# Three more pairs of f tiles begun in the norm of the first feed-forward, their sums kept in DRAM

## The chip, the cores and the metric

The kernel runs on one core of a Trainium2 chip. The metric is the device time of one execution in microseconds (us). The engines are named as in the profile: PE is TensorE, PEld its weight load, DVE is VectorE, ACT is ScalarE, POOL is GpSimd, and SP issues nearly all DMAs; SPq is its queue.

## The reference

The block computes, in float32 for one sequence of 1024 positions with a model width of 1024:

```python
x = x + 0.5 * swiglu(rms_norm(x, ffn1_norm), ffn1_w_gate, ffn1_w_up, ffn1_w_down)
h = rms_norm(x, mix_norm)
x = x + concat(rwkv7_mix(h @ w_in), pool_mix(h @ w_in)) @ w_out
x = x + 0.5 * swiglu(rms_norm(x, ffn2_norm), ffn2_w_gate, ffn2_w_up, ffn2_w_down)
out = rms_norm(x, final_norm)
# swiglu(h, g, u, d) = (silu(h @ g) * (h @ u)) @ d, inner width 2816
```

The change touches the first line only: the norm in front of the first feed-forward and its two products with the gate and the up weights.

## The kernel before

**Tiling.** The inner width of 2816 is cut into 22 f tiles of 128, taken as 11 pairs. For a pair, gate and up are each a product of a 2 x 2 block matrix of weights with a 2 x 2 block matrix of the normed input. It is done with seven block products in place of eight, named P1 to P7. The right sides of the seven are forms of the normed input: `b11` and `b21` (two of its blocks), `b22`, and the sums and differences `t1` to `t4`. Every product is float32 out of two halves: `split` writes a high part with an ACT copy and a low part with a DVE subtraction, and `mm3` (lines 252 to 254) then issues three matmuls for each of four blocks of 128 rows. A product is thus 12 matmuls of 128x512, and a pair takes 14 products.

**Order of a pair.** In `gate_up` the first two products (`first`) need only `b11` and `b21`: P1 is copied out of PSUM by ACT as `c1`, and P2 is added to it by DVE as `c11`. The other five (`rest`) need the other forms and add on to `c1`. `store` then multiplies gate with up on POOL and puts seven tiles of the pair into the DRAM tensor `ascr`, for the down product.

**The norm.** `start` makes the forms of the input, in an order that a planner (`Plan`) writes out for all engines: each operation gets a priority from the length of the chain behind it and from a table `LEAD`, which adds a number for each part of the work. The input `x` is loaded as eight tiles of 512 KB, squared and summed (ACT), transposed (PE, line 845), written back transposed to `xtd`, scaled (line 852, which reads `bc`, the row scales spread over the partitions by PE at line 835), and split. The first 512 positions give `b11` and `b21`, the second 512 give the other forms. In between `start` makes P1 and P2 of the first three pairs (`NPRE`): a weight tile `raw` of 512 KB is loaded by two DMAs (line 728), split into two `wf` tiles (lines 705 and 672), and used by two products on `pp_` accumulators, which take turns in a ring of two PSUM banks; line 735 is the ACT copy and line 737 the DVE add. There are three `raw` buffers, eight `wf` and ten `c`.

**The other norm.** In front of the second feed-forward `start` makes P1 and P2 of six pairs. It keeps the sums of the last three as `c1` and `c11` in the DRAM tensor `c1d` (line 741), and `gate_up` reads them back with `kept` (line 447). Sums of five more pairs were put there earlier, so `gate_up` of the second feed-forward computes five products instead of seven for all of its 11 pairs. The first feed-forward has the argument `a_left` false and does all seven for its last eight pairs.

Of the kernel before, what the change touches and what calls it, by code (L numbers as in the profile page):

```python
# [8 lines left out]
F32 = mybir.dt.float32  # L9
# [7 lines left out]
P = 128  # L17
# [3 lines left out]
NF = DFF // P  # L21
KD = D // P
HT = 512
# [12 lines left out]
class Plan:  # L36
# [148 lines left out]
    def lag(self, i, u):  # L185
# [4 lines left out]

LEAD = {"": 48.5, "1e00": 696.8, "1e01": 905.5, "1e10": -2683.6, "1e11": 2081.2, "1e20": -2679.1, "1e21": -2658.5,
# [15 lines left out]

MANUAL = {mybir.EngineType.PE, mybir.EngineType.DVE, mybir.EngineType.Activation, mybir.EngineType.Pool,  # L210
          mybir.EngineType.SP}
# [3 lines left out]
def block_kernel(ctx, tc, x, ffn1_norm, ffn1_w_gate, ffn1_w_up, ffn1_w_down, mix_norm, w_in,  # L215
# [6 lines left out]
    dram = ctx.enter_context(tc.tile_pool(name="dram", bufs=1, space=DRAM))  # L222
# [100 lines left out]
    NPRE = 3  # L323

    NEARLY = 5
    PROD = ("P1", "P2", "P4", "P6", "P7", "P5", "P3")
    PROD2 = ("P1", "P2", "P3", "P6", "P7", "P5", "P4")

# [2 lines left out]

    def gate_up(fp, rf, begun, wg, wu, ascr, a_left, ahead):

# [115 lines left out]
        for i in range(NF // 2):  # L451
            ahead(i)
            qs = []
            for n, src in enumerate((wg, wu)):
                a = loads(src, i) if i + n else blocks
                if (i, n) in early:
                    c1, q = early[i, n], []
                elif a_left:
                    c1, q = kept(0, i, n), [kept(1, i, n)]
                else:  # L460
                    c1, c11 = first(a)
                    q = [c11]
                q += rest(a, c1, None if i + n else made)
                if n == 0:
                    for c in q:
                        silu(c)
                qs.append(q)
            if i == NF // 2 - 1:
                ahead(i + 1)
            store(i, *qs)  # L470

    TAIL = 3
    NPR = NF // 2
# [167 lines left out]
            split(hi[:, k, :], lo[:, k, :], hf, lo_eng="pool" if k % 2 else "dve")  # L641


    def start(fp, rf, wg, wu, ascr, inputs, pre, through, aside=()):

# [5 lines left out]
        PE, DVE, ACT, POOL, SP = "PE", "DVE", "ACT", "POOL", "SP"  # L651
# [130 lines left out]
    x_v = x[0].rearrange("(i p) d -> p i d", p=P)  # L782
    xtd = dram.tile([NH, P, KD, HT], F32, name="xtd")
    x1d = dram.tile([NH, P, KD, HT], F32, name="x1d")
    ascr = dram.tile([7, NF // 2, P, HT], F32, name="ascr")

    DSC = 4 * (16 * L + 16)
# [12 lines left out]
    with tc.tile_pool(name="f12", bufs=2, side="right", reuse_waits="tile") as fp:  # L800
# [4 lines left out]
        rf = {nm: form(nm) for nm in ("b11", "b21", "b22", "t2", "t3", "t4")}  # L805
# [57 lines left out]
                    else:  # L863
                        rest_ops(k, a, b, "xn0" if k == 0 else "")

        begun = start(fp, right, ffn1_w_gate[0], ffn1_w_up[0], ascr, inputs1, "1", {"PE": 4.4, "ACT": 5.8})

        wb = w_blocks(lambda n: xb.tile([P, 8 * HT], F32, tag="x", name="wx") if n == 0 else xtile("wx", [P, 8 * HT]),
                      ffn1_w_down[0], False)
# [8 lines left out]
                for q in range(3):  # L878
                    load_a(fp, 0, q, PROD)

        gate_up(fp, rf, begun, ffn1_w_gate[0], ffn1_w_up[0], ascr, False, ahead1)

        vec_columns([name for name, _, _ in vecs if name != "g1"])
        omu = const.tile([P, 14], F32, name="omu")
# [32 lines left out]
    xbs.close()  # L917

    x2d = dram.tile([P, KD, HT], F32, name="x2d")
    c1d = dram.tile([2, NF // 2, 2, P, HT], F32, name="c1d")  # L920
    x2n = dram.tile([NH, P, 4, D], F32, name="x2n")
    with tc.tile_pool(name="mix", bufs=1, side="right", reuse_waits="tile") as mp_:

# [882 lines left out]
    with tc.tile_pool(name="f34", bufs=2, side="right", reuse_waits="tile") as fp:  # L1806
        def to_natural(i):

            for q in range(2):
                pt = bank("ptn")  # L1810
                for k in range(4):
                    nc.tensor.transpose(pt[:, k * P:(k + 1) * P], x2[:, q * 4 + k, i * P:(i + 1) * P], ident)
                xs = const.tile([P, HT], F32, tag="sq", name="xs", bufs=3)
                nc.scalar.copy(xs, pt)
                nc.scalar.dma_start(x2n[1, :, i, q * HT:(q + 1) * HT], xs)

        rf3.update({nm: form(nm) for nm in ("b22", "t2", "t3", "t4")})
        rf3["t1"] = xb.tile([P, 2, KH, HT], F32R, tag="x", name="t1")


        fp.tile([P, HT], F32, tag="c", name="c", bufs=10)
        def inputs2(plan, E, alloc, ct, st, sq, sub, split_op, rest_ops):
            op = plan.op
            for k in range(KH):
                plan.part = f"2f{k}"
                hs = []
                for m in (k, k + KH):
                    hf = f"hf{m}"
                    op("DVE", 0.66, lambda m=m, hf=hf: nc.vector.scalar_tensor_tensor(
                        ct(hf), x2[:, m, :], col("g3", m), x2rb, op0=ALU.mult, op1=ALU.mult), "", f"{hf} H", [(hf, "c")])  # L1830
                    hs.append(hf)
                rest_ops(k, *hs, "")

        begun = start(fp, rf3.get, ffn2_w_gate[0], ffn2_w_up[0], ascr, inputs2, "2",
                      {"PE": 8.0, "DVE": 8.0, "ACT": 4.0, "POOL": 4.0}, range(NPRE + NEARLY, NPR))

        wb = w_blocks(lambda n: xtile("wx", [P, 8 * HT]),
                      ffn2_w_down[0], True)

        def ahead2(i):  # L1840
            if 1 <= i <= 4:
                to_natural(i - 1)
            if i >= NPR - 2:
                for _ in range(8 if i == NPR - 2 else 4 if i == NPR else 0):
                    wb[1](*wb[2].pop(0))
            if i == NPR:
                for q in range(3):
                    load_a(fp, 0, q, PROD2)

        gate_up(fp, rf3, begun, ffn2_w_gate[0], ffn2_w_up[0], ascr, True, ahead2)  # L1850

        fg = fp.tile([P, D], F32, tag="raw", name="fg", bufs=3)
        xo = []

        def out2(r, c, m):
            if not xo:
                xo.extend([xtile("xo0", [P, 4, D]), xb.tile([P, 4, D], F32, tag="x", name="xo1")])
                nc.scalar.dma_start(fg, final_norm.rearrange("(a d) -> a d", a=1).broadcast_to([P, D]))
            cs = slice(c * HT, (c + 1) * HT)
            return xo[r][:, m, cs], x2n[r, :, m, cs]  # L1860

        def finish(r, t):
            xs = xo[r][:, t, :]
            s = const.tile([P, 2], F32, tag="s", name="s", bufs=3)
            for q in range(2):
                qs = slice(q * HT, (q + 1) * HT)
                junk = const.tile([P, HT], F32, tag="sq", name="junk", bufs=3)
                nc.scalar.activation(junk, xs[:, qs], AF.Square, accum_out=s[:, q:q + 1])
            nc.vector.tensor_scalar(s[:, 0:1], s[:, 0:1], s[:, 1:2], 1.0 / D, ALU.add, ALU.mult)
            nc.vector.tensor_scalar(s[:, 0:1], s[:, 0:1], RMS_EPS, None, ALU.add)  # L1870
            nc.gpsimd.tensor_tensor(s[:, 0:1], s[:, 0:1], mhalf[:, 0:1], op=ALU.pow)
            nc.vector.scalar_tensor_tensor(xs, xs, s[:, 0:1], fg, op0=ALU.mult, op1=ALU.mult)  # L1872
            r0 = (r * 4 + t) * P
            nc.sync.dma_start(out[0, r0:r0 + P, :], xs)

        def after2(n, m):
            if n == "P5":
                finish(0, m)
            if n == "P4":
                finish(1, m)  # L1880

        down(fp, wb, True, out2, after2)
# [25 lines left out]
```

## Time and profile before

| | |
|---|---|
| median of three runs | 1982.69 us (1980.05 to 1983.21) |
| profiled execution | 1979.47 us, of which the span from first to last instruction is 1977.7 us |
| PE busy in the span | 1860.0 us (94%) |
| DVE, ACT, POOL busy | 1356.7, 814.9, 677.5 us |
| mean granted clock of PE | 0.974 of full speed |

Matmuls are pipelined, so a PE that is busy all the time is shown as busy for the whole of a stretch, and the distance between the starts of two matmuls is what one costs. The busy share is a mean over stages: what is looked for is the stretches where PE is not busy, and there what it waits for. In the stretches the columns are the bounds and length of the stretch, then busy time of PE, PEld, DVE, ACT and POOL with the number of instructions, the granted clock, the mean busy share of the 16 DMA engines, and GB/s. In a timeline a bracket gives the idle time ahead of an instruction and what ended it.

### The profile page before, as it was taken

How to read it: one execution, taken by the hardware profiler on the slowest of the kernel's cores; microseconds unless marked ns; L12 is line 12 of the kernel's file. 1: busy time of each engine (PE TensorE's matmuls, PEld its weight loads, DVE VectorE, ACT ScalarE, POOL GpSimd, SP SyncE). 2: the span in 40 equal slices, each digit the busy share in tenths (PEclk: the TensorE clock that was granted, in tenths of full speed). 3: DMA queues.
4: the chain of work that ended last, by engine and by line, in shares of the span. 5: the costliest groups of instructions: out<-in, count | busy, mean ns of one | idle time of the engine just before them, and what ended most of it. 6: DMA issues, size and time to landing. Idle time of an engine off the chain costs nothing.

```text
span 1977.7 us, 28018 instructions
## 1 busy us (share of the span) xinstructions
PE 1860.0 (94%) x10042; PEld 1478.5 (75%) x10042; DVE 1356.7 (69%) x2299; ACT 814.9 (41%) x1410; POOL 677.5 (34%) x589
## 2 busy tenths in 40 slices
PE   6799999999899998988899998898999999998997
PEld 5588888888678776666677776777788888886886
DVE  7965555556888857677787577456855455589876
ACT  7423333323344455455553445244433222243444
POOL 0375665561631112001310010100266777825300
PEclk9899999999899998989999999999999999998999
DMA  9334333236632342232233437335555655484233
GB/s 286 103 125 131 105 109 102 87 111 230 212 106 93 121 116 61 53 69 59 43 72 94 125 82 207 100 97 177 165 196 174 205 171 180 169 277 132 95 101 128
DMA packets 271532, 260.50 MB, mean 132 GB/s; under 512 B 68318, under 2 KB 197666, under 8 KB 271138
## 3 DMA queue, kind: packets, MB, share of 16 engines
q1 hardware_dynamic: 269952, 256.06, 41.8%
q10 hardware_dynamic: 1442, 2.66, 0.4%
q8 instruction: 80, 1.31, 0.3%
q14 instruction: 58, 0.48, 0.1%
HBM read 186.55 MB, written 71.84 MB: 131 GB/s over the span
## 4 chain that ended last, share of the span: by engine, by line
PE 42%; DVE 6%; ACT 2%; issue 1%; DMA 1%; POOL 0%; SPq 0%; POOLq 0%; DVEq 0%; ACTq 0%
PE pw L252 3%; PE pw L253 3%; PE pw L254 3%; PE pst L1434 1%; DVE da L249 1%; DVE xo L1872 1%; DVE xo L561 0%; PE pz L1409 0%; DVE dw L249 0%; DMA tscr<-ti 0%; PE py L1416 0%; PE sc L1258 0%; PE ptt L1366 0%; DVE xo L601 0%; DVE u L1274 0%
## 5 line engine op out<-in xcount | busy, mean ns | idle before, releaser
L245 ACT ACTIVATE wf<-s 128x512 fp32r<-128x512 f32 x172 | 107.6, 631 | 289.3 <-POOL s L386 87.5
L249 DVE TENSOR_TENSOR wf<-s,wf 128x512 fp32r<-128x512 f32 x172 | 155.8, 906 | 61.7 <-ACT wf L245 59.8
L249 DVE TENSOR_TENSOR dw<-wx,dw 128x512 fp32r<-128x512 f32 x132 | 109.0, 826 | 57.5 <-ACT dw L245 57.4
L245 ACT ACTIVATE dw<-wx 128x512 fp32r<-128x512 f32 x132 | 83.1, 630 | 157.6 <-PE pd__4772 L254 16.9
L249 DVE TENSOR_TENSOR wf<-raw,wf 128x512 fp32r<-128x512 f32 x76 | 78.1, 1028 | 70.7 <-ACT wf L245 69.8
L245 ACT ACTIVATE da<-ar 128x512 fp32r<-128x512 f32 x154 | 95.5, 620 | 43.3 <-DMA ar<-ascr 23.7
L529 POOL TENSOR_TENSOR wx<-wx 128x512 f32<-128x512 f32 x44 | 78.4, 1799 | 100.6 <-DMA wx<-in_ffn_w_down_dram 59.8
L249 DVE TENSOR_TENSOR da<-ar,da 128x512 fp32r<-128x512 f32 x132 | 106.1, 804 | 6.3 <-ACT da L245 6.3
L425 POOL TENSOR_TENSOR c<-c,c 128x512 f32<-128x512 f32 x60 | 98.8, 1647 | 33.4 <-DVE c L353 32.5
L392 POOL TENSOR_TENSOR s<-raw 128x512 f32<-128x512 f32 x44 | 57.2, 1300 | 144.5 <-DMA raw<-in_ffn_w_gate_dram 80.6
L984 DVE TENSOR_TENSOR w<-w 128x512 fp32r<-128x512 f32 (+2 forms) x108 | 70.4, 659 | 18.3 <-ACT w L979 9.8
L979 ACT ACTIVATE w<-w 128x512 fp32r<-128x512 f32 (+2 forms) x108 | 62.6, 595 | 48.0 <-DVE w L984 30.8
L245 ACT ACTIVATE wf<-raw 128x512 fp32r<-128x512 f32 x76 | 47.8, 629 | 78.8 <-DMA vrow<-in_mix_norm_dram 6.3
L386 POOL TENSOR_TENSOR s<-s,raw 128x512 f32<-128x512 f32 x42 | 57.4, 1366 | 34.4 <-DVE wf L249 33.7
L403 POOL TENSOR_TENSOR s<-raw,s 128x512 f32<-128x512 f32 x42 | 54.3, 1292 | 40.6 <-DVE wf L249 35.8
L252 PE MATMUL pw<-h2hi,w 128*128 128x512 f32 (+1 forms) x144 | 62.1, 431 | 2.8 <-ACT w L979 2.8
L252 PE MATMUL pw<-h,w 128*128 128x512 f32 (+1 forms) x144 | 63.3, 439 | 0.0
L254 PE MATMUL pw<-h2hi,w 128*128 128x512 f32 (+1 forms) x144 | 59.1, 411 | 2.1 <-DVE w L984 2.0
L1404 ACT ACTIVATE spt<-sv,ep 128x128 f32<-128x128 f32 x60 | 24.1, 401 | 89.1 <-DVE sv L1441 80.0
L409 ACT ACTIVATE c<-c 128x512 f32<-128x512 f32 x74 | 46.7, 631 | 32.4 <-DVE c L353 27.7
L249 POOL TENSOR_TENSOR da<-ar,da 128x512 fp32r<-128x512 f32 x22 | 32.1, 1461 | 79.7 <-ACT da L245 79.7
L384 POOL TENSOR_TENSOR s<-raw 128x512 f32<-128x512 f32 x42 | 56.5, 1345 | 7.5 <-DMA raw<-in_ffn_w_up_dram 2.0
(3084 smaller groups left out, 5935.7 us busy)
## 6 DMA issues: line engine op xcount, KB each, us to landing
ar<-ascr SPq DMA_DIRECT2D x70, 512.0 KB
ascr<-c SPq DMA_DIRECT2D x132, 256.0 KB
raw<-in_ffn_w_gate_dram SPq DMA_DIRECT2D x44, 512.0 KB
wx<-in_ffn_w_down_dram SPq DMA_DIRECT2D x88, 256.0 KB
raw<-in_ffn_w_up_dram SPq DMA_DIRECT2D x44, 512.0 KB
w<-in_w_in_dram SPq DMA_DIRECT2D x64, 256.0 KB
ck<-c1d SPq DMA_DIRECT2D x32, 256.0 KB
w<-in_w_out_dram SPq DMA_DIRECT2D x26, 256.0 KB
```

The source lines that it names most:

```text
L245: nc.scalar.activation(hi, src, AF.Copy)
L249: eng.tensor_tensor(lo, src, hi.bitcast(F32), op=ALU.subtract)
L252: nc.tensor.matmul(acc, lhsT=lhi, rhs=rhi, start=first, stop=False)
L253: nc.tensor.matmul(acc, lhsT=lhi, rhs=rlo, start=False, stop=False)
L254: nc.tensor.matmul(acc, lhsT=llo, rhs=rhi, start=False, stop=last)
L384: nc.gpsimd.tensor_tensor(s1, a21, a22, op=ALU.add)
L386: nc.gpsimd.tensor_tensor(s2, s1, a11, op=ALU.subtract)
L392: nc.gpsimd.tensor_tensor(s3, a11, a21, op=ALU.subtract)
L425: eng.tensor_tensor(u[j], u[j], g[j], op=ALU.mult)
L529: eng.tensor_tensor(out, a, b, op=op)
L979: nc.scalar.activation(part(t, q, kn), by32(raw), AF.Copy)
L984: nc.vector.tensor_tensor(part(E[f"l{w}"], q, kn), by32(raw), part(E[f"h{w}"], q, kn).bitcast(F32), op=ALU.subtract)
```

## The change

P1 and P2 of the pairs 3, 4 and 5 (`NASIDE` = 3) of the first feed-forward are made by `start` as well. Their sums go to a new DRAM tensor `c0d` of the shape of `c1d`, and `gate_up` reads them back with `kept` for these three pairs; the pairs 6 to 10 still do seven products there. The table `LEAD` has new numbers for the parts of the first norm (the names that begin with 1), so the order of all engines is new up to the pair 6; behind it the order on each engine is that of before, but for line numbers and buffer numbers. The instructions of PE, DVE, ACT and POOL are as many as before. SP issues 36 DMAs more, of 256 KB each: 12 loads of weights (the columns of P1 and P2 of the six weight tiles, which `gate_up` loads whole again later), 12 stores to `c0d` and 12 loads from it.

```diff
-LEAD = {"": 48.5, "1e00": 696.8, "1e01": 905.5, "1e10": -2683.6, "1e11": 2081.2, "1e20": -2679.1, "1e21": -2658.5,
+LEAD = {"": 48.5, "1e00": 1988.1, "1e01": 2891.4, "1e11": -36.8, "1e20": -64.8, "1e21": -450.3, "1e30": 1.9,
...
+    NASIDE = 3
...
-    def gate_up(fp, rf, begun, wg, wu, ascr, a_left, ahead):
+    def gate_up(fp, rf, begun, wg, wu, ascr, a_left, ahead, aside, c1d):
...
-                elif a_left:
+                elif i in aside:
                     c1, q = kept(0, i, n), [kept(1, i, n)]
                 else:
                     c1, c11 = first(a)
...
-    def start(fp, rf, wg, wu, ascr, inputs, pre, through, aside=()):
+    def start(fp, rf, wg, wu, ascr, inputs, pre, through, aside, c1d):
...
+    c0d = dram.tile([2, NF // 2, 2, P, HT], F32, name="c0d")
...
-        begun = start(fp, right, ffn1_w_gate[0], ffn1_w_up[0], ascr, inputs1, "1", {"PE": 4.4, "ACT": 5.8})
+        begun = start(fp, right, ffn1_w_gate[0], ffn1_w_up[0], ascr, inputs1, "1", {"PE": 4.4, "ACT": 5.8},
+                      range(NPRE, NPRE + NASIDE), c0d)
...
-        gate_up(fp, rf, begun, ffn1_w_gate[0], ffn1_w_up[0], ascr, False, ahead1)
+        gate_up(fp, rf, begun, ffn1_w_gate[0], ffn1_w_up[0], ascr, False, ahead1, range(NPRE, NPRE + NASIDE), c0d)
```

**First place: SP at the start of the program.** The first loads stand there; `raw` is a weight tile, `xn` the input. Before:

```order
L728 DMA raw<-in_ffn_w_up_dram 128x4x128 x2
L817 DMA xn_106<-in_x_dram 128x1024 x4
L728 DMA raw<-in_ffn_w_up_dram 128x4x128 x2
L728 DMA raw<-in_ffn_w_gate_dram 128x4x128 x2
L817 DMA xn_107<-in_x_dram 128x1024 x2
```

In the change:

```order
L824 DMA xn_108<-in_x_dram 128x1024 x4
L732 DMA raw<-in_ffn_w_up_dram 128x4x128 x2
L824 DMA xn_109<-in_x_dram 128x1024 x3
L858 DMA xtd<-sq 128x512 x3
L824 DMA xn_109<-in_x_dram 128x1024
```

The first four tiles of the input now stand ahead of the first weights, and the loads of two further weight tiles behind the second half of the input.

**Second place: DVE where it comes to the second half of the input.** `bc_313` and `bc_465` are the row scales of that half, `sq` is a transposed tile, `wf` is a weight split, and L737 (now L741) adds a product `pp`. Before:

```order
L672 TENSOR_TENSOR b21_111<-st_309,b21_111 128x512
L672 TENSOR_TENSOR wf_298<-raw_243,wf_298 128x512
L852 SCALAR_TENSOR_TENSOR c_354<-sq_339,vt_86,bc_313 128x512
L672 TENSOR_TENSOR wf_307<-raw_243,wf_307 128x512
L672 TENSOR_TENSOR st_365<-c_354,st_333 128x512
L672 TENSOR_TENSOR wf_350<-raw_254,wf_350 128x512
```

In the change:

```order
L676 TENSOR_TENSOR c_373<-c_373,c_403 128x512
L676 TENSOR_TENSOR wf_417<-raw_365,wf_417 128x512
L676 TENSOR_TENSOR wf_431<-raw_381,wf_431 128x512
L676 TENSOR_TENSOR wf_451<-raw_400,wf_451 128x512
L741 TENSOR_TENSOR c_428<-pp__423,c_428 128x512
L859 SCALAR_TENSOR_TENSOR c_479<-sq_339,vt_86,bc_465 128x512
L676 TENSOR_TENSOR wf_472<-raw_381,wf_472 128x512
L676 TENSOR_TENSOR st_490<-c_479,st_394 128x512
```

The first operation on the second half stood behind the splits of seven `wf` tiles; now 14 such splits and the adds of three products stand ahead of it. On PE the matmuls that make `bc_465` stand behind seven whole products in the change, and the first of them that reads `bc_465` here comes next on DVE.

**Third place: DVE at the end of the norm.** `t2`, `t3` and `t4` are forms, `wf_623` and `wf_875` the weight of the first product of the five that need them; the next rows (L249, now L250) belong to `gate_up`. Before:

```order
L672 TENSOR_TENSOR t2_113<-c_588,t2_113 128x512
L672 TENSOR_TENSOR wf_430<-raw_304,wf_430 128x512
L672 TENSOR_TENSOR t4_115<-st_593,t4_115 128x512
L737 TENSOR_TENSOR c_608<-pp__562,c_559 128x512
L672 TENSOR_TENSOR st_610<-raw_370,raw_408 128x512
L672 TENSOR_TENSOR st_617<-st_610,raw_370 128x512
L672 TENSOR_TENSOR c_535<-c_535,c_608 128x512
L672 TENSOR_TENSOR wf_623<-st_617,wf_623 128x512
L249 TENSOR_TENSOR wf_673<-s3_671,wf_673 128x512
```

In the change:

```order
L676 TENSOR_TENSOR st_684<-st_684,c_718 128x512
L676 TENSOR_TENSOR wf_775<-raw_724,wf_775 128x512
L676 TENSOR_TENSOR t4_117<-st_684,t4_117 128x512
L676 TENSOR_TENSOR st_849<-b21_113 128x512
L676 TENSOR_TENSOR st_849<-st_849,c_749 128x512
L741 TENSOR_TENSOR c_859<-pp__835,c_840 128x512
L676 TENSOR_TENSOR t4_117<-st_849,t4_117 128x512
L676 TENSOR_TENSOR st_870<-st_802,raw_492 128x512
L676 TENSOR_TENSOR wf_875<-st_870,wf_875 128x512
L250 TENSOR_TENSOR wf_915<-s3_913,wf_915 128x512
L250 TENSOR_TENSOR wf_933<-raw_553,wf_933 128x512
L741 TENSOR_TENSOR c_893<-pp__877,c_881 128x512
```

Before, a `wf` of an early product, the last, was split between the last forms, and the adds of two early P2 stood behind the rows shown. In the change the last early weight (from `raw_724`) is split ahead of the last `t4`, and of the adds of the 12 early P2 only the last, of `pp__877`, stands behind `wf_875`.

## Rows read from the trace of the kernel before

**Rows 1.** Page, part 1: busy us (share of the span) xinstructions.

```profile
PE 1860.0 (94%) x10042; PEld 1478.5 (75%) x10042; DVE 1356.7 (69%) x2299; ACT 814.9 (41%) x1410; POOL 677.5 (34%) x589
```

**Rows 2.** Stretches of 10 us of the first feed-forward's norm. Columns: TensorE to GpSimd, clock, DMA.

```profile
0.00:10.00 10.00, 1.19 (x3) 0.54 (x3) 3.36 (x44) 4.40 (x6) 0.83 (x7) 1.00 0.78 244
10.00:20.00 10.00, 6.97 (x34) 6.44 (x34) 4.57 (x8) 9.02 (x18) 1.03 (x1) 1.00 1.06 326
20.00:30.00 10.00, 8.90 (x48) 6.53 (x49) 10.00 (x18) 9.06 (x18) 1.02 (x1) 1.00 1.04 329
...
50.00:60.00 10.00, 8.43 (x34) 5.90 (x33) 10.00 (x18) 4.36 (x8) 0.00 (x0) 1.00 0.15 53
60.00:70.00 10.00, 1.93 (x9) 1.22 (x7) 10.00 (x17) 3.60 (x6) 0.00 (x0) 0.76 0.14 52
70.00:80.00 10.00, 8.43 (x26) 6.43 (x27) 9.06 (x11) 4.01 (x8) 5.98 (x5) 0.72 0.62 186
80.00:90.00 10.00, 10.00 (x45) 8.02 (x44) 9.27 (x11) 4.43 (x8) 5.96 (x5) 1.00 0.47 131
```

**Rows 3.** Stretches of the two gate and up stages, same columns.

```profile
100.00:500.00 400.00, 400.00 (x1712) 322.02 (x1712) 229.53 (x304) 125.06 (x204) 219.35 (x156) 1.00 0.39 128
1510.00:1734.00 224.00, 224.00 (x966) 180.33 (x965) 124.77 (x168) 64.70 (x111) 173.73 (x120) 1.00 0.55 183
```

**Rows 4.** Timeline of TensorE, norm of the first feed-forward. Columns: start us, us, engine line op.

```profile
35.42 1.04 PE L845 MATMUL pt<-ident,xn 128*128 128x128 f32 x8
...
61.54 0.40 PE L254 MATMUL pp__562<-b,wf 128*128 128x512 f32 x1
70.81 0.79 PE L252 MATMUL pp__613<-b,wf 128*128 128x512 f32 x1 [8.87 <-DVE c L737]
...
76.53 0.40 PE L252 MATMUL pp__676<-t,wf 128*128 128x512 f32 x1
77.70 0.50 PE L252 MATMUL pp__635<-b,wf 128*128 128x512 f32 x1 [0.77 <-ACT c L735]
...
80.61 0.40 PE L252 MATMUL pp__656<-t,wf 128*128 128x512 f32 x1
...
85.30 0.39 PE L252 MATMUL pp__694<-t,wf 128*128 128x512 f32 x1
...
88.11 0.40 PE L252 MATMUL pp__712<-t,wf 128*128 128x512 f32 x1
```

**Rows 5.** Timeline of VectorE, the same norm.

```profile
17.58 1.41 DVE L852 SCALAR_TENSOR_TENSOR st<-sq,vt,bc 128x512 f32<-128x512 f32 x2 [1.25 <-PE bc L835]
...
25.75 0.68 DVE L672 TENSOR_TENSOR b<-st,b 128x512 fp32r<-128x512 f32 x1
...
30.15 0.68 DVE L672 TENSOR_TENSOR b<-st,b 128x512 fp32r<-128x512 f32 x1
...
33.54 0.68 DVE L672 TENSOR_TENSOR st<-c,st 128x512 f32<-128x512 f32 x1
...
70.07 0.68 DVE L737 TENSOR_TENSOR c<-pp__562,c 128x512 f32<-128x512 f32 x1
...
73.47 0.69 DVE L672 TENSOR_TENSOR wf<-st,wf 128x512 fp32r<-128x512 f32 x1
```

**Rows 6.** Timeline of all engines, the first loads.

```profile
0.81 1.00 SPq L728 DMA_DIRECT2D raw<-in_ffn_w_up_dram  x2
...
3.82 0.63 ACT L705 ACTIVATE wf<-raw 128x512 fp32r<-128x512 f32 x1 [0.69 <-DMA raw<-in_ffn_w_up_dram]
...
11.93 1.06 ACT L822 ACTIVATE t<-xn 128x1024 fp32r<-128x1024 f32 x1 [0.20 <-DMA xn<-in_x_dram]
```

**Rows 7.** Timeline of TensorE, norm of the second feed-forward.

```profile
1357.52 0.80 PE L252 MATMUL pp__12004<-b,wf 128*128 128x512 f32 x1 [5.03 <-ACT wf L705]
...
1425.96 0.50 PE L252 MATMUL pp__12549<-b,wf 128*128 128x512 f32 x1 [1.12 <-DVE c L737]
...
1428.87 0.40 PE L252 MATMUL pp__12568<-t,wf 128*128 128x512 f32 x1
```

More of the change, by code (lines that the diff above doesn't have):

```diff
@@ L784, in block_kernel @@
     x1d = dram.tile([NH, P, KD, HT], F32, name="x1d")
+    c0d = dram.tile([2, NF // 2, 2, P, HT], F32, name="c0d")
+    c1d = dram.tile([2, NF // 2, 2, P, HT], F32, name="c1d")
     ascr = dram.tile([7, NF // 2, P, HT], F32, name="ascr")
@@ L919, in block_kernel @@
     x2d = dram.tile([P, KD, HT], F32, name="x2d")
-    c1d = dram.tile([2, NF // 2, 2, P, HT], F32, name="c1d")
     x2n = dram.tile([NH, P, 4, D], F32, name="x2n")
@@ L1834, in block_kernel @@
         begun = start(fp, rf3.get, ffn2_w_gate[0], ffn2_w_up[0], ascr, inputs2, "2",
-                      {"PE": 8.0, "DVE": 8.0, "ACT": 4.0, "POOL": 4.0}, range(NPRE + NEARLY, NPR))
+                      {"PE": 8.0, "DVE": 8.0, "ACT": 4.0, "POOL": 4.0}, range(NPRE + NEARLY, NPR), c1d)
         wb = w_blocks(lambda n: xtile("wx", [P, 8 * HT]),
@@ L1848, in ahead2 @@
                     load_a(fp, 0, q, PROD2)
-        gate_up(fp, rf3, begun, ffn2_w_gate[0], ffn2_w_up[0], ascr, True, ahead2)
+        gate_up(fp, rf3, begun, ffn2_w_gate[0], ffn2_w_up[0], ascr, True, ahead2, range(NPRE, NPR), c1d)
         fg = fp.tile([P, D], F32, tag="raw", name="fg", bufs=3)
```

31 rows, old and new, of the table LEAD are left out of this document.

## The prediction

> **What bounds the kernel now.** I read the page's first part, then stretches, then the timelines of PE and DVE where a stretch has a hole. PE is busy 1860.0 us of the span [rows 1]; what can be gained is in the rest and in slow clock. In the gate and up stage of the first feed-forward PE is busy 400.00 of 400.00 us [rows 3]: there each product that is taken out shortens the program by what a product costs. That is 2.81 us, from the start of `pp__694` at 85.30 to that of `pp__712` at 88.11 [rows 4]; 12 matmuls at 400 us for 1712 [rows 3] are 2.804; I reckon with 2.805. In the norm ahead of it the picture is the other way round. From 50 to 80 us DVE is busy 29.06 of 30 us, PE 18.79 [rows 2]; PE waits 8.87 us for a DVE add ahead of `pp__613`, and the granted clock is 0.76 and 0.72 in the two stretches around that hole [rows 2, 4], with matmuls of 0.79 us where others take 0.40 [rows 4].
>
> I measure the norm by what PE has lost by its end: the time less 2.805 us for each product done. At 80.61 us, when `pp__656`, the first product whole on a new form, starts and PE has no more holes [rows 2 to 4], 12 early products and 4 of the 12 matmuls of `pp__676` (the last of them at 76.53 [rows 4]) are done: 80.61 - 12.33 x 2.805 = **46.0 us lost**.
>
> **What the change does.** Nothing is removed in sum. 12 products (12 x 2.805 = 33.7 us of PE) move from a stage that PE bounds into one where it waits. With them go 12 high and 12 low weight halves, 6 ACT copies and 6 DVE adds, from a stage where DVE is busy 229.53 of 400 us [rows 3] into one that DVE bounds. In the norm DVE issues a row each 0.619 us (59 rows of its order from 33.54 to 70.07 [rows 5]), so 18 more DVE operations are 11.1 us. If DVE alone bound the norm, the gain would be 33.7 - 11.1 = 22.6 us. But PE now has 67.3 us of early products to do there, so I follow both.
>
> *Start.* The four first input tiles now stand ahead of the first weight tile, whose DMAs were issued at 0.81 us [rows 6]. ACT was released by the last of these tiles at 11.93 [rows 6], and the first scaling on DVE came at 17.58, having waited for PE's `bc` [rows 5]. The weight tile is 0.52 MB, at 244 GB/s [rows 2] 2.1 us. Bounds: 0 us; and 4.0 us, if none of the weight bytes had to pass first (2.44 MB by 10 us and 0.63 MB at 326 GB/s by 11.93, less 2.10 MB of input, is 0.97 MB). I take 2.1, since only one weight tile stood wholly ahead: scaling starts at 15.5.
>
> *Forms.* From the first scaling to the last split of `b11` DVE needs 13 rows, to that of `b21` 21, as many as before, where they took 8.17 us (to 25.75) and 12.57 us (to 30.15) [rows 5]. So `b11` is whole at 24.4 and `b21` at 28.8. PE then finishes its first product (0.7), does a second (2.8), four blocks of transposes (1.04 us for two [rows 4], so 2.1), half a product (1.4) and one more (2.8): four products are done at 34.2. None of this waits for `b21`.
>
> *PE to the end.* 20 products remain, 56.1 us, and the second `bc` and a transposed block, an estimate of 1.5 us from the 1.04 us for two blocks. Without a wait the 24th product ends at 91.8.
>
> *DVE to the end.* It can't begin the second half before `bc`, which stands behind the seventh product on PE: 34.2 + 8.4 + 1.0 = 43.6. Queued behind it are all remaining forms and, with them, weights of later products. From there to `wf_875` are 71 rows, 44.0 us: 87.6, and 88.3 with the last row. PE wants that weight at 91.8. So DVE is 3.5 us ahead: both engines are nearly full to the end, and PE is the one that ends last. The DMA waits fall into the cover of this margin; without it each us late on DVE is a us late at the end.
>
> *Waits.* The norm of the second feed-forward does the same thing already, 24 early products, three pairs set aside, DVE full. From 1357.52 to 1428.87, where its first new-form product starts whole, are 71.35 us for 24.33 products, 68.3 us [rows 7]: 3.1 us lost, of which 1.1 is a wait for a DVE add and the rest a cold clock at the start (its first matmul took 0.80 us [rows 7]). That is the lower bound, 1.1 us. For the upper one I take the first norm as it was: from 35.42 to the last matmul of `pp__562` at 61.54, so to 61.78, PE did 8 products in 26.4 us in place of 22.4 [rows 4], 0.49 a product with three blocks of transposes; for 20 products 9.8, less the 1.5 counted above, 8.3 us. I take 2.0, near the second norm, whose early products were as many and whose DVE was as full.
>
> *Sum.* The 24th product ends at 93.8, so 93.8 - 67.3 = 26.5 us are lost in place of 46.0: **19.5 us gained**. Behind it the pairs 0 to 2 run as before. For the pairs 3 to 5 `kept` puts four 0.26 MB loads a pair on SP's queue between the weight loads; DVE reads them for the first add of five. The second feed-forward does that for all 11 pairs: PE busy 224.00 of 224.00 us at a DMA share of 0.55 [rows 3]. So this costs nothing; what hides it is the PSUM ring and a DMA share that was 0.39 here [rows 3]. From pair 6 the order is the old one and simply comes earlier.
>
> The profiled execution took 1979.47 us; less 19.5 it is 1960.0. The median of the runs is 3.2 us higher, and from it I forecast **1963 us**. 0.2% (4 us) is about what a measurement of this kernel can tell from no change.
>
> **The rivals.**
>
> *PE waits at every product.* If PE goes on waiting for the evacuation of the product ahead, as it did (8.87 and 0.77 us are the two waits shown [rows 4]), at the upper bound above, the gain is 19.5 - 6.3 = 13.2 us: 1969.5. For it: in-order DVE and a ring of two banks, and adds planned by a model. Against it: [rows 7].
>
> *The loads bound the norm.* From 10 to 30 us the DMA share is 1.06 and 1.04 at 326 and 329 GB/s [rows 2], so it is full there, and 6.3 MB more (3.1 of weights, 3.1 of sums) go into the norm. Up to the last early weight I count 20.7 MB; at 326 GB/s that is 63 us, at 244 GB/s [rows 2] 85, and PE wants the weight, split, at 91.8 less two products, 86.2. From 50 to 70 us only 52 to 53 GB/s flowed [rows 2]. So at the lowest rate seen under load it is a us or two late, at the others far ahead. At 200 GB/s it would be 104 us, 18 to 19 late, and the gain about 1 us: 1982, no change. The Trainium skill, "Perfetto Trace Analysis", section "DMA Optimizations", says that DMAs under 2 KB have a significant overhead for each transfer, which speaks against this change, since its weight loads come in runs of 512 bytes; it gives no price for these. The 326 and 329 GB/s were reached with the same kind of loads among the others, so I give it little.
>
> *Slower: the last three weights starve PE.* The two tiles of pair 0 that `gate_up` will need take two of the three `raw` buffers in the middle of the norm. The last three early weight tiles then pass one after the other through the third: a load (3.0 us from 0.81 to 3.82 [rows 6]), two ACT and two DVE splits in their places in the queues, and only then the next load, on an SP queue that also waits for stores of sums and for PE's last transposes. PE uses such a tile in two products, 5.6 us. If a turn takes d us more, PE stops for 3d; from d = 6.5, a turn of 12.1 us, nothing is gained, and at 13.5 us the kernel takes 1987. Against it: on DVE the splits of these tiles are 12 rows (7.4 us) and more apart, but were done well ahead of PE by my times (the first at 59 us, for a product that starts at 75).
>
> *Nothing comes out:* the moved products come back as waits for the kept sums in the pairs 3 to 5. It would take 1.6 us of wait at each of 12 loads: 1982. [rows 3] speak against it.
>
> **How the numbers follow.** My forecast, a gain of 15 to 22.3 us: 0.75; waits at every product, 8 to 15 us: 0.14; loads or kept sums that eat nearly all, half of it within 0.2%: 0.06; slower: 0.05. The bounds give gains of 19.5 + 1.9 + 0.9 = 22.3 us (1960) and 19.5 - 2.1 - 6.3 = 11.1 us (1972); as the runs of before spread by 3 us, the range is 1958 to 1972. Faster by over 0.2%: 0.92; within: 0.03; slower: 0.05.
>
> **What the profile will show.** Right: 24 products on `b11` and `b21` ahead of the first one on `t2`, which starts at about 94 us, PE full from about 25 us at a granted clock of 1.00, no hole like the 8.87 us; five products a pair and a full PE for pairs 0 to 5; gate and up ending about 19 us earlier, and all behind it shifted by that. Wrong: a first `t2` product beyond 100 us, with DVE waiting for `raw` or PE for DVE adds in the brackets; or PE waits ahead of the adds of `ck`.

## The result

| | before | with the change |
|---|---|---|
| median | 1982.69 us (3 runs) | 1962.45 us (4 runs, 1956.57 to 1964.52) |
| ratio, 95% interval | | 0.9893 [0.9875, 0.991] |
| profiled execution, span | 1979.47, 1977.7 us | 1964.52, 1962.8 us |

The kernel became 20.2 us faster in the median (17.8 to 24.8 by the interval). 1963 us was forecast, with 1958 to 1972 as the range.

**The page.** Part 1 of the page of the changed kernel answers to [rows 1]: as many instructions, busy times nearly the same, on a span that is 14.9 us shorter.

```profile
PE 1857.3 (95%) x10042; PEld 1477.9 (75%) x10042; DVE 1353.5 (69%) x2299; ACT 812.2 (41%) x1410; POOL 673.9 (34%) x589
```

**The norm in stretches.** The same 10-us stretches of the changed kernel as in [rows 2]; columns are busy time of PE, PEld, DVE, ACT, POOL with instruction counts, granted clock, DMA share, GB/s.

```profile
0.00:10.00 10.00, 3.17 (x12) 2.29 (x13) 2.15 (x43) 6.33 (x11) 0.99 (x8) 1.00 0.82 290
10.00:20.00 10.00, 7.75 (x47) 6.78 (x46) 7.17 (x12) 9.00 (x18) 0.87 (x1) 1.00 1.07 334
20.00:30.00 10.00, 8.69 (x46) 6.37 (x45) 9.37 (x17) 8.02 (x16) 0.00 (x0) 1.00 0.87 277
...
50.00:60.00 10.00, 10.00 (x47) 8.08 (x46) 9.32 (x16) 6.51 (x12) 0.00 (x0) 1.00 0.81 264
60.00:70.00 10.00, 9.77 (x42) 7.58 (x41) 9.96 (x17) 5.89 (x10) 0.00 (x0) 1.00 0.95 322
70.00:80.00 10.00, 10.00 (x44) 8.04 (x43) 10.00 (x17) 6.25 (x12) 0.00 (x0) 1.00 0.57 176
80.00:90.00 10.00, 10.00 (x45) 8.02 (x44) 8.74 (x14) 3.75 (x7) 1.67 (x1) 1.00 0.26 81
```

Between 60 and 70 us PE now does 42 matmuls at full clock where it did 9 at 0.76. DVE is as full as it was, and the DMA share there went from 0.14 to 0.95. So PE, DVE and the loads are all nearly full at the same time.

**Matmuls done.** A simple measure of the norm is the count of PE's matmuls in the first 130 us, since PE is full from about 90 us in both kernels. First the row of the kernel before.

```profile
0.00:130.00 130.00, 102.83 (x440) 80.15 (x441) 100.91 (x184) 64.94 (x110) 40.80 (x37) 0.96 0.58 180
```

The same stretch of the changed kernel:

```profile
0.00:130.00 130.00, 119.37 (x532) 95.56 (x533) 101.52 (x191) 69.81 (x120) 35.67 (x31) 1.00 0.68 213
```

92 more, at 400 us for 1712 [rows 3] 0.2336 us each: 21.5 us. Behind gate and up that is still there: the first down product starts 21.6 us earlier (its first ACT split of `dw` at 437.88 in place of 459.48 us).

**Gate and up**, stretches of both feed-forwards, as in [rows 3]: still full, with the loads of kept sums in it.

```profile
110.00:480.00 370.00, 370.00 (x1585) 297.92 (x1584) 218.49 (x290) 114.28 (x189) 224.96 (x160) 1.00 0.45 149
1490.00:1714.00 224.00, 224.00 (x966) 180.32 (x965) 123.03 (x167) 64.52 (x110) 173.70 (x121) 1.00 0.55 181
```

**Where the norm's times come from.** The timeline of PE in the changed kernel, answering to [rows 4]: two of the early products, and the first product on `t2`.

```profile
30.98 0.40 PE L253 MATMUL pp__369<-b,wf 128*128 128x512 f32 x1
...
33.79 0.39 PE L253 MATMUL pp__396<-b,wf 128*128 128x512 f32 x1
...
91.81 0.40 PE L253 MATMUL pp__898<-t,wf 128*128 128x512 f32 x1
```

The timeline of DVE in the changed kernel, answering to [rows 5]: the first scaling, the first one of the second half, and the weight of that product on `t2`.

```profile
14.13 1.41 DVE L859 SCALAR_TENSOR_TENSOR st<-sq,vt,bc 128x512 f32<-128x512 f32 x2 [1.04 <-PE bc L842]
...
43.31 0.75 DVE L859 SCALAR_TENSOR_TENSOR c<-sq,vt,bc 128x512 f32<-128x512 f32 x1 [1.36 <-PE bc L842]
...
89.05 1.00 DVE L676 TENSOR_TENSOR wf<-st,wf 128x512 fp32r<-128x512 f32 x1 [0.70 <-ACT wf L709]
```

The timeline of ACT in the changed kernel, the first four input tiles, as the last row of [rows 6]:

```profile
4.37 1.06 ACT L829 ACTIVATE t<-xn 128x1024 fp32r<-128x1024 f32 x1 [1.27 <-DMA xn<-in_x_dram]
...
8.40 1.06 ACT L829 ACTIVATE t<-xn 128x1024 fp32r<-128x1024 f32 x1 [0.17 <-DMA xn<-in_x_dram]
```

What decides the start are the first loads. Both kernels from 2.00 to 8.40 us, before and then with the change:

```profile
2.00:8.40 6.40, 0.58 (x2) 0.36 (x2) 2.43 (x37) 2.75 (x4) 0.00 (x0) 1.00 0.96 280
2.00:8.40 6.40, 1.59 (x4) 0.72 (x4) 1.06 (x35) 4.55 (x7) 0.00 (x0) 1.00 0.98 362
```

The waits of PE from 20 to 130 us in the changed kernel: what waited for what, us in total, times, the longest.

```profile
PE pt L852 <- ACT sq L857: 1.0, 1, 1.0
PE pp__640 L253 <- DVE c L741: 0.2, 1, 0.2
PE pp__213 L254 <- DVE b L676: 0.2, 1, 0.2
```

The 8.87 us wait of [rows 4] is gone and nothing took its place. 24 products are done at 91.81 us, so 91.81 - 24 x 2.805 = 24.5 us are lost in place of 46.0.

**What was given back.** Yet the span is only 14.9 us shorter. From the first `dw` of the first down product to the first `wf` of the second norm (ACT's rows at 437.88 and 1341.05 us) are 903.2 us, where before it was 897.4. A stretch of 80 us that begins 17 us behind that first `dw` shows most of it, here in the kernel before:

```profile
477.00:557.00 80.00, 72.45 (x293) 57.40 (x292) 67.20 (x83) 29.20 (x53) 42.04 (x22) 0.94 0.63 214
```

The same 80 us, 22 us earlier, in the changed kernel:

```profile
455.00:535.00 80.00, 69.31 (x273) 54.34 (x272) 67.82 (x82) 29.03 (x52) 35.87 (x22) 0.91 0.65 216
```

20 matmuls fewer are 4.7 us. Neither kernel is near the 342 that 0.2336 us each would give in 80 us (`e9_before_dve` below has 355). The timeline of DVE in the changed kernel shows why:

```profile
502.74 0.68 DVE L607 TENSOR_SCALAR x<-pd__3818 128x512 f32<-128x512 f32 x1
503.34 0.68 DVE L250 TENSOR_TENSOR dw<-wx,dw 128x512 fp32r<-128x512 f32 x1
503.94 0.68 DVE L250 TENSOR_TENSOR da<-ar,da 128x512 fp32r<-128x512 f32 x1
504.55 1.76 DVE L565 TENSOR_TENSOR x<-x,res 128x512 f32<-128x512 f32 x1
506.23 1.77 DVE L250 TENSOR_TENSOR dw<-wx,dw 128x512 fp32r<-128x512 f32 x1
```

The timeline of POOL, same place:

```profile
504.46 2.98 POOL L533 TENSOR_TENSOR wx<-wx 128x512 f32<-128x512 f32 x2 [9.39 <-DMA wx<-in_ffn_w_down_dram]
```

POOL starts at 504.46, and from then on the DVE operations take 1.76 us in place of 0.68. PE waits for these splits (`pd__4046` for `da`, 10.7 us in six waits), and its granted clock falls to 0.91 in the mean of these 80 us.

### The profile page after: what moved, and what is told of

It reads as the page before. It is cut to its first block, busy times and chain, and to the rows that moved or that the text cites. A ratio compares the mean times of both kernels' runs of the same rounds, so it can differ in the third digit from the quotient of the medians.

```text
span 1962.8 us, 28065 instructions
## 1 busy us (share of the span) xinstructions
PE 1857.3 (95%) x10042; PEld 1477.9 (75%) x10042; DVE 1353.5 (69%) x2299; ACT 812.2 (41%) x1410; POOL 673.9 (34%) x589
## 4 chain that ended last, share of the span: by engine, by line
PE 42%; DVE 6%; DMA 2%; ACT 2%; issue 1%; POOL 0%; SPq 0%; POOLq 0%; DVEq 0%; ACTq 0%
PE pw L253 3%; PE pw L254 3%; PE pw L255 3%; DVE xo L1879 1%; DVE dw L250 1%; DVE xo L565 0%; PE pst L1441 0%; PE pz L1416 0%; DVE da L250 0%; DMA tscr<-ti 0%; PE py L1423 0%; PE ptt L1373 0%; PE pq L1373 0%; PE sc L1265 0%; DMA hf<-x2d 0%
## 5 line engine op out<-in xcount | busy, mean ns | idle before, releaser
L250 DVE TENSOR_TENSOR wf<-s,wf 128x512 fp32r<-128x512 f32 x172 | 163.9, 953 | 78.6 <-ACT wf L246 77.2
L250 DVE TENSOR_TENSOR dw<-wx,dw 128x512 fp32r<-128x512 f32 x132 | 108.2, 820 | 60.2 <-ACT dw L246 60.1
L250 DVE TENSOR_TENSOR da<-ar,da 128x512 fp32r<-128x512 f32 x132 | 105.8, 802 | 6.6 <-ACT da L246 6.5
L250 DVE TENSOR_TENSOR wf<-raw,wf 128x512 fp32r<-128x512 f32 x64 | 61.8, 965 | 65.3 <-ACT wf L246 64.5
L533 POOL TENSOR_TENSOR wx<-wx 128x512 f32<-128x512 f32 x44 | 72.1, 1657 | 99.0 <-DMA wx<-in_ffn_w_down_dram 69.5
L390 POOL TENSOR_TENSOR s<-s,raw 128x512 f32<-128x512 f32 x42 | 58.5, 1392 | 24.8 <-DVE wf L250 23.8
L250 POOL TENSOR_TENSOR da<-ar,da 128x512 fp32r<-128x512 f32 x22 | 32.1, 1460 | 91.8 <-ACT da L246 91.8
L246 ACT ACTIVATE wf<-raw 128x512 fp32r<-128x512 f32 x64 | 40.1, 626 | 51.0 <-PE pp__12598 L255 3.3
```

Of the source, the lines that this page charges most:

```text
L246: nc.scalar.activation(hi, src, AF.Copy)
L250: eng.tensor_tensor(lo, src, hi.bitcast(F32), op=ALU.subtract)
L390: nc.gpsimd.tensor_tensor(s2, s1, a11, op=ALU.subtract)
L533: eng.tensor_tensor(out, a, b, op=op)
```

## The experiments

Each was timed against the kernel before on the same chip; the ratio is to that, and the runs are compared with one another by their ratios. A count of matmuls is of the first 130 us of the profiled execution. The change itself, run again (`e4_again`), had 0.9895 [0.9882, 0.9909].

**The new order alone: `e1_none`.** No pair is set aside, the table is the new one.

```diff
-    NASIDE = 3
+    NASIDE = 0
```

> The changed kernel with NASIDE = 0: the new table of priorities alone, no pair set aside, gate and up of the pairs 3 to 5 do seven products again. Theory (the gain is the 12 products moved into PE's holes): the norm is then bound by DVE; from the first scaling to the first t2 weight DVE has 93 rows, at 0.619 us each and with a wait of some 2.5 us for the second bc, so the first t2 product starts near 75 us with 12 early products done, 41.8 us lost against 46.0 before; the time is 1978 to 1980 us, 3 to 5 us under the kernel before, all of it from the earlier loads of x. Rival (the new order alone brings the gain): 1962 us, with 24 to 26 us lost.

Measured: 1981.38 us, ratio 0.9982 [0.9971, 0.9993], so 3.6 us faster (1.4 to 5.7), as the theory had it. 444 matmuls, four more than before, are 0.9 us, and the first `dw` comes 0.9 us earlier (458.61 us): in this trace only so much of the gain lies in the norm. The longest of PE's waits there:

```profile
PE pp__612 L255 <- DVE wf L676: 12.1, 1, 12.1
```

The first product on `t2` starts at 77.99 us. With nothing to do in the hole, PE waits 12.1 us at once for DVE. The order alone brings little; the rival is out.

**One pair: `e2_one`** (`NASIDE` = 1).

> NASIDE = 1: one pair set aside. Theory: each pair moved while DVE bounds the norm gives 4 x 2.805 = 11.2 us of PE less 6 DVE rows, 3.7 us, so 7.5 us a pair: 34.3 us lost at the first t2 product, 1971 us. Rival (the new order alone): 1962 us, as with three pairs.

Measured: 1977.58 us, 0.9952 [0.994, 0.9965], 9.5 us faster where 11.7 were expected; 471 matmuls, 27 more than with no pair, so 6.3 us for the pair in place of 7.5. The timeline of PE shows what is left of the hole, ahead of the first product on `t2`:

```profile
81.19 0.79 PE L253 MATMUL pp__738<-t,wf 128*128 128x512 f32 x1 [10.63 <-ACT wf L709]
```

**Four pairs: `e3_four`** (`NASIDE` = 4).

> NASIDE = 4: a fourth pair is set aside (the table has no numbers for its parts, they get 0). Theory: with three pairs PE is already full from 24 us on, so a fourth moves 11.2 us from one full stage into another: first t2 product near 103 us with 28 products done, 24 to 26 us lost, the time within 2 us of the kernel with three pairs. Rival (every pair gives the same 6.7 us, a third of 20.2): 1956 us. Second rival (the loads bound the norm from here on): PE waits for DVE or for raw tiles, 1966 us or more.

Measured: 1963.37 us, 0.9895 [0.9879, 0.991]; 522 matmuls, the first product on `t2` at 105.45 us. As much as with three: the hole is full, and a fourth pair only moves work from one full stage to another. In matmuls the first pair brought 27, the second and third together 55 to 61 (6.4 to 7.1 us a pair, by the two traces with three pairs), the fourth none.

**The change again: `e4_again`.**

> The changed kernel unaltered, for a second profile and for the time beside the other runs of this call. In the first profile the first t2 product started at 91.81 us, 21.5 us less lost than before, but the end came only 14.9 us earlier; 5 to 6 us were given back between 500 and 550 us, in the first down product, where DVE's subtractions take 1.7 us in place of 0.68 while POOL is busy. Theory (what is given back there differs from execution to execution): the first t2 product again at 91.8 us within 0.5, the end of gate and up at the same place, and another loss in the down product; median 1959 to 1964 us. Rival (a loss that belongs to the change): the same 5 to 6 us given back at the same place.

Measured: 1964.69 us, 0.9895 [0.9882, 0.9909]; 526 matmuls, the first product on `t2` at 93.44 us, with PE waiting 1.4 us for one DVE add. So the times in the norm differ by 1.6 us between executions of one program. The add is the one ahead of `pp__640`, for which PE waited 0.2 us in the first trace: it waits for the store of a kept sum, 1.9 us here and 0.7 there. The theory on the down product failed, and the rival holds for these two traces: the same loss lies in the same place, with 270 matmuls in its 80 us (273 in the first trace).

**The old table: `e5_old_table`.** The table of before, to which only the numbers of the new parts (1e30 to 1e51) are added; three pairs are set aside as in the change.

> Three pairs set aside, but all old numbers of the table stay; only the parts of the three new pairs get the numbers of the change. Two weight tiles (1.05 MB) then stand ahead of the first input tiles, and six of eight weight tiles ahead of the second half. Theory (moving the products is the gain, the table only places them): PE is full from some 5 us later than in the change (1.05 MB at 244 GB/s is 4.3 us), 29 to 31 us are lost, the time is 14 to 17 us under the kernel before. Rival (the new numbers are what makes room): PE waits again in the norm and less than 8 us are gained.

Measured: 1980.52 us, 0.9992 [0.998, 1.0005]: at most 4 us gained. 453 matmuls, 13 more than before, are 3.0 us. The same products are made by the same code, and do not fall into the holes. The theory failed, the rival came true. Some of PE's waits from 14 to 130 us:

```profile
PE pp__545 L252 <- DVE c L740: 3.1, 1, 3.1
PE pp__235 L252 <- ACT b L681: 1.8, 2, 1.2
PE pp__235 L253 <- DVE b L675: 1.6, 4, 0.7
PE pt L851 <- DVE sq L854: 1.1, 1, 1.1
```

And two of its stretches:

```profile
20.00:30.00 10.00, 6.48 (x25) 3.90 (x25) 5.35 (x10) 7.50 (x15) 0.00 (x0) 1.00 0.95 324
50.00:60.00 10.00, 5.80 (x24) 4.06 (x23) 8.84 (x16) 4.59 (x8) 0.00 (x0) 1.00 0.88 280
```

The first scaling is back at 17.53 us, and DVE, which was full here in the kernel before, has 4.65 idle us from 20 to 30. PE gets 25 matmuls where it had 48 [rows 2]. So with these two tables neither the moved products nor the order does it alone; the gain needs both.

**Sums made again: `e6_seven`.** The norm is that of the change, but `gate_up` does all seven products of the pairs 3 to 5 and doesn't read the kept sums.

```diff
-        gate_up(..., ahead1, range(NPRE, NPRE + NASIDE), c0d)
+        gate_up(..., ahead1, (), c0d)
```

> The change, but gate_up doesn't read the kept sums and makes P1 and P2 of the pairs 3 to 5 again (the sums in c0d are written and not used). Theory: the norm is that of the change and costs what it costs, the gate and up stage, which PE bounds, gives nothing back: 33.7 us over the change, so some 13 us over the kernel before. Rival (the gate and up stage has hidden waits that five products only uncover): clearly less than 30 us over the change.

Measured: 1997.65 us, 1.0075 [1.0047, 1.0102]. The change's 0.9895 of the same 1982.23 us is 1961.4, so +36 us with some 6 us of uncertainty. The traces show it more closely: the first `dw` comes at 472.84 us, 33.3 and 35.0 us behind those of the two traces of the change (439.51 and 437.88). That is the 33.7 us of 12 products, as the prediction priced them.

**Sums stored twice: `e7_twice`.** The change, with a second store of each kept sum to a tensor that nobody reads.

```diff
+                                nc.sync.dma_start(c1e[d, i, n], E[c1])
```

> The change with every kept sum stored twice, the second time into a tensor that nobody reads: 12 DMAs of 256 KB more in the norm. Theory (the DMAs lie beside full PE and DVE): within 2 us of the change. Rival (the loads and stores bound the norm): 3.1 MB at 326 GB/s are 9.6 us, so 5 to 10 us over the change, with PE or DVE waiting for raw tiles.

Measured: 1968.42 us, 0.9926 [0.9902, 0.9951], 6 us over the change. 498 matmuls, 28 to 34 fewer than in the two traces of the change, which is 6.5 to 7.9 us. The waits of DVE from 40 to 80 us:

```profile
DVE c L741 <- DMA c1e<-c: 5.9, 3, 3.6
DVE wf L676 <- ACT wf L709: 2.5, 4, 1.1
```

In the change there is one such wait, and it is short:

```profile
DVE c L741 <- DMA c0d<-c: 0.7, 1, 0.7
```

The second product's add works in place on `c`, the tile that the stores still read, so it waits for them, here for the second one; and PE waits 4.4 us for the add, with a granted clock of 0.77 and 0.89 in the two stretches of 10 us from 60 us on. 12 more stores of 256 KB, 3.1 MB, were enough for that; the first `dw` comes 6.4 and 8.0 us later than in the two traces of the change. The theory failed; the rival had the size right, but what DVE waited for was a store and not a `raw` tile.

**POOL's work moved to DVE, first down product: `e8_down_dve`.** The change, with the 22 differences and sums of weight quarters (`forms0`) on DVE.

```diff
-                tt_(nc.gpsimd, ap(0, i), ap(0, i), ap(2, i), ALU.subtract)
-                tt_(nc.gpsimd, ap(2, i), ap(2, i), ap(3, i), ALU.add)
+                tt_(nc.vector, ap(0, i), ap(0, i), ap(2, i), ALU.subtract)
+                tt_(nc.vector, ap(2, i), ap(2, i), ap(3, i), ALU.add)
```

> The change, with the 22 subtractions and adds that make the weight forms of the first down product on DVE instead of POOL. In both kernels DVE's splits take 1.7 us in place of 0.68 while POOL does these, PE waits 7 to 11 us for them and its clock falls. Theory (POOL and DVE hold each other up there, and this is where executions differ): DVE needs 4 x 0.6 = 2.4 us for each of 11 steps in which PE needs 2.8, PE waits less, 4 to 9 us under the change and a smaller spread. Rival (DVE is the bound of that stage anyway): 22 x 0.6 = 13 us more on DVE, 3 to 10 us over the change.

Measured: 1948.89 us, 0.9828 [0.9805, 0.9852], 13 us less than the change, more than the theory had; the rival is out. The stretch of 80 us:

```profile
455.00:535.00 80.00, 79.52 (x351) 65.38 (x350) 70.07 (x122) 38.26 (x68) 0.00 (x0) 1.00 0.71 239
```

DVE does 122 instructions in 70.07 us in place of 82 in 67.82; by its groups from 495 to 535 us, splits and forms alike take 685 ns.

```profile
L250 DVE TENSOR_TENSOR da<-ar,da 128x512 fp32r<-128x512 f32 x16 | 11.0, 685 | 0.0
L533 DVE TENSOR_TENSOR wx<-wx 128x512 f32<-128x512 f32 x13 | 8.3, 685 | 0.0
```

78 matmuls more than in the change are 18 us; from `dw` to the second norm are 884.8 us (439.54 to 1324.37) in place of 903.2.

**The same without the change: `e9_before_dve`.**

> The kernel before, without the change, with one edit: the 22 differences and sums of weight quarters ahead of the first down product are made on DVE in place of POOL (nothing is left out). Theory, that DVE operations of 0.68 us become 1.7 us wherever POOL works on tiles beside them, and that this cost stood in the kernel before too: the stage from the first down product to the mixer shrinks from 244.6 us to 228 to 232, and the time falls by about 13 us, to a ratio of 0.993 to 0.994, so that the gain of this edit and that of the change simply add. Rival, that the change itself brought the collision (the first down product now starts on weights that arrive in another order): at most 3 us, a ratio above 0.998.

Measured: 1965.73 us, 0.9908 [0.9894, 0.9923], so 18 us off the kernel before. The 80 us from 477 us on, where it had 293 matmuls:

```profile
477.00:557.00 80.00, 80.00 (x355) 66.16 (x354) 71.39 (x125) 38.94 (x70) 0.00 (x0) 1.00 0.70 236
```

The collision stood in the kernel before too; the 13 expected were too few.

**Both down products: `e10_both_dve`.**

> The change, with the forms of weight quarters of both down products on DVE in place of POOL: 22 operations in the first, as in the run before, and 22 in the second (nothing is left out). Theory, that POOL's work beside DVE costs in the second down product what it cost in the first: between 1755 and 1785 us DVE was busy 30.00 of 30 us with 128x512 operations of 1.46 to 1.74 us, and PE 25.52; in the 50 us from 1760 PE lost 6.3. With POOL away they take 0.68 us and PE fills: 4 to 6 us less than with the first down product alone, a ratio of 0.980. Rival, that the loads of these weights set the pace there (POOL waited 11.3 us for them in those 30 us): within 1.5 us of the first alone, a ratio of 0.982 to 0.984.

Measured: 1929.03 us, 0.9725 [0.9708, 0.9742], 20 us less than with the first alone and the fastest of all. In the traces it is 16 us, from the first `wf` of the second norm to the end (607.4 us in place of 623.4). A stretch of 50 us of the second down product in `e8_down_dve`, where POOL still made the forms:

```profile
1742.00:1792.00 50.00, 42.03 (x153) 31.40 (x152) 49.47 (x49) 16.63 (x30) 31.40 (x19) 0.90 0.45 155
```

The same with DVE making them:

```profile
1742.00:1792.00 50.00, 50.00 (x222) 41.42 (x221) 47.05 (x78) 22.22 (x41) 0.00 (x0) 1.00 0.52 180
```

The rival, that loads set the pace, is out. My 4 to 6 us were wrong too: the 69 matmuls missing are 16.1 us, and I had counted PE's idle time (8.0 us here). About 24 of the matmuls that do run start 0.43 us apart where the others start 0.23 apart (granted clock 0.90 in the mean), which is some 4.7 us more. Most of the rest is that a matmul ahead of a wait is shown as busy for 0.39 to 0.50 us, where the next could have started after 0.23.

## Why the prediction was right

**What bounds the kernel, and the price of a product:** right. `e6_seven` gave 36 us for 12 products (33.3 and 35.0 by the traces) where 33.7 were reckoned, gate and up stayed full, and the kept loads cost nothing at a DMA share of 0.45.

**Start:** mis-sized. The fourth input tile landed 3.5 us earlier (8.40 for 11.93 us), not 2.1, near the upper bound of 4.0, and the first scaling came at 14.13 for a forecast of 15.5. The prediction counted bytes at one rate. Fewer came first, 2.34 MB by 8.40 us (279 GB/s) where it had been 3.11 MB by 11.93 (261 GB/s), and they also moved faster: 362 GB/s from 2.00 to 8.40 us, nine tenths of it input, in place of 280 with weights among them. Most of the surplus was lost again on the forms: from the first scaling to the start of the last split of `b21` are 13.98 us where 12.57 were taken over from before, and four products were done at 33.79 for a forecast of 34.2.

**PE and DVE to the end:** right. The second half started at 43.31 (43.6). DVE began the weight at 89.05 (87.6) and was done with it at 90.05 (88.3), so it was 1.8 us ahead of PE and not 3.5. PE ended at 91.81, which is the forecast without waits; the 2.0 us taken for waits were 0.4 from 20 us on, apart from the 1.0 at a transpose, and 1.4 in the repetition, which ended at 93.4 (93.8). The gain in the norm was 21.5 and 20 us for a forecast of 19.5. PE was full from about 24 us on, as said.

**What the sum rests on, and the text passed over:** the order. It was read for where things stand, and the new table's part in the gain got no term. `e5_old_table` shows that with the old order the gain is 4 us at most, `e1_none` that the new one is worth 3.6 us by itself. My later belief that the table only places the new parts fell.

**The rivals.** *PE waits at every product* didn't happen. *The loads bound the norm* didn't happen either, but it was nearer than the prediction had it, which put the loads "far ahead" at the rates of the trace: it counted bytes, those of the sums among them, and not that a DVE add waits for a store; `e7_twice` shows that 3.1 MB more cost 6 us. The prediction also gave little to the weight loads' runs of 512 bytes. The trace of the change shows a price: from 30 to 40 us, when eight of the ten DMAs issued are weight loads, 262 GB/s at a DMA share of 0.90, against the 362 at 0.98 from 2.00 to 8.40 us, when nine tenths was input in rows of 4 KB.

```profile
30.00:40.00 10.00, 10.00 (x44) 8.03 (x43) 7.72 (x13) 5.34 (x8) 1.99 (x1) 1.00 0.90 262
```

That is about a fifth less for the same share, though no run varied the length of the runs alone. The Trainium skill, "Perfetto Trace Analysis", section "DMA Optimizations", warns of an overhead of small transfers, and these rows agree; it did not decide this change, since PE was full. *The last weights starve PE* and *the kept sums wait*: no such wait in the trace.

**"All behind it shifted by that":** wrong. Of the 21.5 us, 5.8 were lost between the first down product and the second norm, 4.7 of them in the 80 us shown. Two traces of the change agree on this (903.2 and 902.5 us for this part), but it is not a fixed price of the change: the other six kernels with POOL's forms there (`e1_none` to `e3_four`, `e5_old_table` to `e7_twice`) have 892.5 to 901.7 us, the kernel before 897.4. The three with the forms on DVE have 881.3, 883.5 and 884.8. What is shown is that the collision of POOL and DVE lies there and costs 16 to 18 us by this part of the traces; why this part is 5 to 6 us longer in the two traces of the change than in that of before was not settled.

**The total:** the median came out 0.6 us from the forecast because two errors cancel, which is luck. The forecast put the median 3.2 us above the profiled execution; in the changed kernel the profiled execution, at 1964.52 us, is the slowest of the four, 4.5 us above the 1960.0 forecast for it, and the median is 2.1 us below it.

## What to carry to other kernels

Work moved into a stage where an engine waits pays only if its place in every queue lets it fall into the hole, so a change of contents and a change of order are to be tried apart and together. Count matmuls in a fixed stretch: it takes in waits and slow clock at once, where idle time alone missed half of the loss. When one operation has two durations in a trace, look at what the other engines do at that moment before tuning anything else: here that was worth some 34 us (0.9895 to 0.9725), against some 20 for the change that was studied.

## What the runs showed of the hardware

A DVE operation on two 128x512 float32 tiles in SBUF takes 0.68 us alone and 1.76 beside POOL operations of the same shape, which take 1.65 us in the mean of the 22 in the stretch of 80 us. A DVE add with one of its inputs in PSUM keeps its 0.68 us. DVE in gate and up of the changed kernel, a split and such an add:

```profile
93.93 1.77 DVE L250 TENSOR_TENSOR wf<-s,wf 128x512 fp32r<-128x512 f32 x1
95.63 0.68 DVE L357 TENSOR_TENSOR c<-pp__898,c 128x512 f32<-128x512 f32 x1
```

POOL at the same time:

```profile
93.51 1.64 POOL L388 TENSOR_TENSOR s<-raw 128x512 f32<-128x512 f32 x1 [0.65 <-DVE wf L250]
95.23 1.63 POOL L390 TENSOR_TENSOR s<-s,raw 128x512 f32<-128x512 f32 x1
```

It is not always DVE that is held up. In the kernel before, ten DVE operations in a row, the first and last of them shown, kept 0.68 us while one POOL operation is shown as 7.69 us long:

```profile
527.89 7.69 POOL L529 TENSOR_TENSOR wx<-wx 128x512 f32<-128x512 f32 x1 [10.84 <-DVE dw L249]
528.33 0.68 DVE L561 TENSOR_TENSOR x<-x,res 128x512 f32<-128x512 f32 x1
...
533.75 0.68 DVE L561 TENSOR_TENSOR x<-x,res 128x512 f32<-128x512 f32 x1
```

Whether that is why the kernel before lost less there was not tested.

The Trainium skill, "SBUF — State Buffer", section "SBUF: two separate sides", says that a DVE operation with two SBUF inputs and a GpSimd operation that reads SBUF share a pair of ports as an exclusive lock, each blocked while the other has it; these rows agree, and so does the add out of PSUM, which is not slowed. "Perfetto Trace Analysis" of the same skill, section "Optimizing Scalar/DVE Operations", concludes that moving work between the two might not help. Here it did, by 18 us in the kernel before (`e9_before_dve`) and by 16 to 20 in the second down product, for 22 operations each: on POOL one takes 1.65 us and holds up DVE, on DVE it takes 0.69.
